# State-space factors held without their empty halves and multiplied in 64 by 64 pieces; attention's near and far values joined by a transpose and an addition

## The chip, the cores and the metric

One core of a Trainium2 chip runs the whole kernel. The metric is the device time of one execution in microseconds (us), taken as the median of several. The core has five engines that work through their own queues of instructions in order: PE (TensorE, matrix products; the loading of its weights is listed apart as PEld), DVE (VectorE), ACT (ScalarE), POOL (GpSimd) and SP (which here only issues transfers). Products go into PSUM, a memory of eight banks of 128 by 512 fp32 numbers, and DVE and ACT copy them out.

## The reference, cut to what matters

One block of a hybrid network on 512 tokens of width 1024, in fp32:

```
z = rms_norm(x) @ w_in                       # state-space input, q, k, v, two gates
y_a = s5_mixer(z[:, :512]) @ w_branch_a      # 32 groups of 16 channels, 64 complex states each
y_b = dilated_attention(q, k, v) @ w_branch_b
h = x + (g_a * y_a + g_b * y_b) @ w_out
h = h + conv-gated feed-forward(h);  h = h + per-layer gate(h, p);  return rms_norm(h)

# s5_mixer: per group g and state p, with a = exp(lambda * dt)
s[t] = a * s[t-1] + bbar @ u[t]              # complex
y[t] = Re(c @ s[t]) + d * u[t];  y = gelu(y);  y = y * sigmoid(y @ glu_w + glu_b)

# dilated_attention: 12 heads in three groups; a query's output joins, over the three groups,
# sums of exp(score) * value over the last 128 tokens, over every 4th and over every 16th token
```

## The kernel before, in words

**Layout.** The 512 tokens are held as four residues (token modulo 4) of 128. The large products are done in fp32r as three products, high by high, high by low and low by high part (`mm3`, L149 to L151; 3168 products of 128x128 weights, nearly all by 512 columns). Their weights come in chunks of 128x1024 over SP's queue; ACT makes the high part (`wh`, L128) and DVE the low part (`wl`, L129), three buffers each.

**The background work.** Two generators, `g_ssm` (state space) and `g_attn` (attention), issue their instructions between the large products; after every few products `tick` lets them go on for a budget of estimated cost, which each `yield` states. A scheduler with priorities then fixes each engine's order when the program is built, so on the chip each queue is a fixed list. Small products of both take PSUM tiles of one bank from a pool of three (`ax_tile`); the large ones have five more.

**State space.** Tokens are taken in 128 blocks of four. The 32 groups stand in 16 pairs; a pair's two groups of 64 states fill 128 partitions. The factors of the recurrence within a block are built on DVE (`expand`): `BD[i]` (i is the real or imaginary plane) maps a pair's inputs (2 groups by 4 taps by 16 channels) to its states. As one group's inputs do not touch the other group's states, half of each 128x128 factor is zero; POOL writes the zeros (`zero`, L587) and ACT copies the two filled 64-row halves in (L601). Then on PE:

- `g1t` (L616): 32 transposes of `BD`, 128x128 each, copied by ACT to `G1` (L617).
- `hps` (L627): 32 products of `BD` with the output factors, 128x32 weights by 128 columns, which give the response within a block; DVE copies them (L628), four transposes `hp` turn them, DVE adds them to the direct term `Hm`, and three products `shp` (L645) shift them to make the matrix `T`.
- `ut` (L658): 16 transposes of the input, copied by ACT to `U`.
- `es` (L671): 32 products of `G1` with `U`, 128x128 by 128 columns, the input's share of each block's end state; ACT copies each bank in two pieces to `E`, one block late (L673, L674).
- DVE then runs the recurrence over the 128 blocks in place in `E` (`cstep`; it also rebuilds the factors as `G2`).
- `ys` (L721 to L723): per pair three products, `U` by `T` and `E` by both planes of `G2`, then gelu on ACT.

**Attention.** Eight steps of two heads and 128 queries, each followed by 24 large products of the gates (`gps`): scores (L766, L771), softmax on DVE and ACT, transposes of the probabilities (L796, L798). The values of the two sparse groups come out with queries on partitions (`values`, L817; DVE copies them to `ao`), those of the near group with channels on partitions (`far_values`, L828). `finish_values` (L834) multiplies `ao` by the identity and lets PSUM add it to the near values; ACT and DVE then split the sum into its high and low parts `bh` and `bl`.

After `ys`, the attention and the gates the rest is large products in a row, with no background work.

Of the kernel before, what the change touches and what calls it, by code (L numbers as in the profile page):

```python
# [17 lines left out]
P = 128  # L18
# [3 lines left out]
R = 4  # L22
NQ = 16
H = 16
# [40 lines left out]
def tile_hybrid_block(ctx: ExitStack, tc: tile.TileContext, xT, xtok, pT, W, vecs, consts, ssm, out):  # L65
    nc = tc.nc
    ACT, DVE, POOL, PE = nc.scalar, nc.vector, nc.gpsimd, nc.tensor
# [4 lines left out]
    ring = ctx.enter_context(tc.tile_pool(name="ring", bufs=3))  # L72
# [3 lines left out]
    def slot(i, shape, name, dt=F32):  # L76
        return sb.tile([P] + shape, dt, tag=f"s{i}", name=name)
# [7 lines left out]
    def ax_tile(name):  # L85
        return px.tile([P, 512], F32, tag="ax", name=name)
# [105 lines left out]
    ident = cst[:, C_ID:C_ID + 128]  # L192
# [231 lines left out]
    def g_ssm():  # L424
# [123 lines left out]
        for e in range(2, 5):  # L548
            o = (pn(), pn())
# [30 lines left out]
        ncim = pz[:, 4]  # L580
        Hm = pz[:, 5]
# [4 lines left out]
        def zero(t):  # L586
            POOL.memset(t, 0.0)  # L587

        def expand(dst, ex, plane, e0, re, im, sgn):
# [7 lines left out]
            tt(w[:, 1], imb, pi if plane == 0 else pr, ALU.mult)  # L597
            tt(w[:, 0], w[:, 0], w[:, 1], ALU.subtract if plane == 0 else ALU.add)
# [8 lines left out]
        BD = [slot(f"g{i}", [NQ, 2, R, H], f"BD{i}") for i in range(2)]  # L607
        G1 = [slot(f"f{i}", [NQ, P], f"G1{i}") for i in range(2)]
        for i in range(2):
            zero(BD[i])  # L610
            yield from expand(BD[i], ex, i, 1, bb[:, 0], bb[:, 1], 1.0)
        for i in range(2):
            for q4 in range(4):
                ps = ax_tile("g1t")
                for q in range(4):
                    PE.transpose(ps[:, q * 128:(q + 1) * 128], flat(BD[i], q4 * 4 + q), ident)  # L616
                ACT.activation(G1[i][:, q4 * 4:q4 * 4 + 4, :].rearrange("p q m -> p (q m)"), ps, AF.Copy)  # L617
                yield 0.15


        hT = slot("U", [4, P], "hT")
        hps = ax_tile("hps")
        for q in range(NQ):
            q0 = min(q, NQ - 2)
            o = hps[(q % 4) * 32:(q % 4) * 32 + 32, (q // 4) * 128:(q // 4 + 1) * 128]
            for i, cc in enumerate((c_re, ncim)):
                PE.matmul(o, cc[:, q0:q0 + 2, :].rearrange("p q h -> p (q h)"), flat(BD[i], q), start=(i == 0), stop=(i == 1))  # L627
# [5 lines left out]
        hv = hp2.rearrange("p (q h) -> p q h", h=32)  # L633
        tt(Hm, cst[:, C_DI:C_DI + 16].unsqueeze(1).to_broadcast([P, NQ, H]), sp[:, S_D:S_D + 16].unsqueeze(2).to_broadcast([P, NQ, H]), ALU.mult)
        tt(Hm[:, 0:15], Hm[:, 0:15], hv[:, 0:15, 0:16], ALU.add)
        tt(Hm[:, 15:16], Hm[:, 15:16], hv[:, 15:16, 16:32], ALU.add)
        T = slot("T", [NQ, 2, R, H], "T")
        zero(T)
        Hf = Hm.rearrange("p q h -> p (q h)")
# [11 lines left out]

        while "s_done" not in env:
            yield None
        U = slot("U", [NQ, P], "U")
        for q4 in range(4):
            ps = ax_tile("ut")
            for q in range(4):
                PE.transpose(ps[:, q * 128:(q + 1) * 128], flat(S, q4 * 4 + q), ident)  # L658

            ACT.activation(U[:, q4 * 4:q4 * 4 + 4, :].rearrange("p q (i b) -> p q i b", i=4),  # L660
                           ps.rearrange("p (q b i) -> p q i b", q=4, i=4), AF.Copy)
            yield 0.15
        E = slot("x", [2, NQ, P], "E")
        E4 = E.rearrange("p i q (f b) -> p i q b f", f=4)
        E16 = E.rearrange("p i q (f s g) -> p i q s g f", f=4, g=4)
        DVE.memset(E[:, :, :, 0:1], 0.0)
        for i in range(2):
            for q4 in range(4):
                ps = ax_tile("es")
                for q in range(4):  # L670
                    PE.matmul(ps[:, q * 128:(q + 1) * 128], G1[i][:, q4 * 4 + q, :], U[:, q4 * 4 + q, :], start=True, stop=True)  # L671
                psq = ps.rearrange("p (q c) -> p q c", q=4)
                ACT.activation(E[:, i, q4 * 4:q4 * 4 + 4, 32:128], psq[:, :, 0:96], AF.Copy)  # L673
                ACT.activation(E[:, i, q4 * 4:q4 * 4 + 4, 1:32], psq[:, :, 96:127], AF.Copy)  # L674
                yield 0.15

        G2 = [slot(f"g{i}", [NQ, 2, R, H], f"G2{i}") for i in range(2)]
        ex2 = slot("f1", [2048], "ex2")
# [36 lines left out]
        Yg = slot("S", [R, 32, H], "Yg")  # L715
        for q4 in range(4):
            ps = ax_tile("ys")
            for q in range(4):
                qq = q4 * 4 + q
                o = ps[:, q * 128:(q + 1) * 128]  # L720
                PE.matmul(o, U[:, qq, :], flat(T, qq), start=True, stop=False)  # L721
                PE.matmul(o, E[:, 0, qq, :], flat(G2[0], qq), start=False, stop=False)
                PE.matmul(o, E[:, 1, qq, :], flat(G2[1], qq), start=False, stop=True)  # L723
# [14 lines left out]
    def g_attn():  # L738
# [83 lines left out]
        def far_values(n, ov, pT_):  # L822
            t, hp = n // 2, n % 2
            nb = 2 if t else 1
            for b in range(nb):
                for a in range(2):
                    h = 2 * hp + a
                    PE.matmul(ov[halves[a], 0:128], V[:, t - nb + 1 + b, h * 64:(h + 1) * 64], pT_[:, a, 2 + b, :],  # L828
                              start=(b == 0), stop=False, skip_group_check=True)

        def finish_values(n, ov, ao):

            t, hp = n // 2, n % 2
            PE.matmul(ov[:, 0:128], ao, ident, start=False, stop=True, skip_group_check=True)  # L834
            ov3 = ov[:, 0:128].rearrange("p (r i) -> p r i", r=R)
            bhv, blv = tile_of(bh[:, hp], t), tile_of(bl[:, hp], t)
            ACT.activation(bhv, ov3, AF.Copy)
            tt(blv, ov3, bhv.bitcast(F32), ALU.subtract)

# [85 lines left out]
    h = slot("x", [KD, SEQ], "h")  # L925
# [25 lines left out]
    for m in range(KD):  # L951
        ps = mm_tile("ops")
# [10 lines left out]
    for part in range(2):  # L963
# [4 lines left out]
        for mi in range(HALF):  # L968
# [23 lines left out]
        for m in range(KD):  # L992
            ps = mm_tile("dps")
# [13 lines left out]
    for m in range(KD):  # L1007
        ps = mm_tile("pps")
# [31 lines left out]
    for m in range(KD - NLAST):  # L1040
        ps = mm_tile("eps")
# [48 lines left out]
    n = 0  # L1090
    for rs, y in zip(LAST, y4):
        for j in range(2):
            for r in rs:
# [3 lines left out]
                o = fo[r // 2][:, r % 2, j * 512:(j + 1) * 512]  # L1097
# [52 lines left out]
def _layout(inputs):  # L1150
# [22 lines left out]
    def add(t):  # L1173
        parts.append(t.transpose(1, 0, 2).reshape(128, -1))
# [3 lines left out]
    def tok(c0, n):  # L1178
        add(w_in[:, c0:c0 + n].reshape(8, 128, n))

    tok(0, 512)
    tok(2304, 512)
    for j in range(3):
        tok(512 + 512 * j, 512)
# [34 lines left out]
    dd = np.broadcast_to(f["ssm_d"][0].reshape(16, 2, 1, 16), (16, 2, 4, 16)).reshape(16, 128).T  # L1219
# [26 lines left out]
```

## Time and profile before

| | us |
|---|---|
| median of 3 runs | 797.88 (796.67 to 797.92) |
| profiled execution, its own time | 797.59 |
| its span, first to last instruction | 795.8 |
| PE busy in the span | 786.5 (99%) |
| DVE busy | 494.1 (62%) |
| ACT busy | 346.5 (44%) |

The page's first part gives busy time by engine, its second part the span in 40 slices of 19.9 us with the busy share in tenths. An fp32 product appears in PE's records as two records, a transpose and an fp32r product as one. Records overlap, since a product is some 0.16 us or more in the array after the next has begun: what a product takes of PE's time is the distance from its start to the next one's start, not the length of its record.

### The profile page before, as it was taken

To read this page: it belongs to the slowest core of one execution; us is meant where nothing else is said; L and a number is where in the kernel's file an instruction comes from. 1 tells how busy PE (TensorE), PEld (TensorE's weight loads), DVE (VectorE), ACT (ScalarE), POOL (GpSimd) and SP (SyncE) were. 2 spreads that over 40 slices of the span, in tenths; PEclk is the share of its full clock that TensorE was granted. 3 is DMA by queue.
4 is the path that set the end of the run, shared out by engine and by line. 5 is a ranking of instruction groups with operands and counts; after the bars stand their busy time and mean duration, and the time that the engine had idled before them with its cause. 6 is when DMAs were issued, how large, how long until landed. Compare 5 with 4: busy or idle time off the path is not lost.

```text
span 795.8 us, 10898 instructions
## 1 busy us (share of the span) xinstructions
PE 786.5 (99%) x4302; PEld 650.6 (82%) x4302; DVE 494.1 (62%) x960; ACT 346.5 (44%) x551; POOL 10.9 (1%) x10
## 2 busy tenths in 40 slices
PE   8999999999999999999999999999999999999996
PEld 6888888888777788888888888888888888888886
DVE  6974799943566558656856555233566565455576
ACT  5763643445445443435534433212334333335464
POOL 2001000000000000000000000000000000000000
PEclk9999999999999999999999999999999999999999
DMA  7731122231121122633222332332322322322302
GB/s 268 272 104 54 54 80 80 81 107 54 61 73 55 54 105 83 209 106 110 103 98 87 107 103 82 106 102 84 106 89 97 106 95 90 106 91 94 106 1 107
DMA packets 23811, 78.99 MB, mean 99 GB/s; under 512 B 2640, under 2 KB 3024, under 8 KB 23760
## 3 DMA queue, kind: packets, MB, share of 16 engines
q1 hardware_dynamic: 23616, 78.22, 28.9%
q8 instruction: 34, 0.56, 0.3%
q14 instruction: 17, 0.14, 0.1%
q10 hardware_dynamic: 144, 0.07, 0.0%
HBM read 76.18 MB, written 2.10 MB: 98 GB/s over the span
## 4 chain that ended last, share of the span: by engine, by line
PE 94%; ACT 2%; DVE 2%; issue 1%; DMA 1%; SPq 0%; DVEq 0%; ACTq 0%
PE pg L151 5%; PE dps L151 5%; PE pu L151 5%; PE dps L150 5%; PE pu L150 5%; PE pu L149 5%; PE pg L150 5%; PE pg L149 5%; PE dps L149 5%; PE pa L151 4%; PE pa L150 4%; PE pa L149 4%; PE gps L149 4%; PE gps L151 4%; PE gps L150 4%; PE ops L151 2%
## 5 line engine op out<-in xcount | busy, mean ns | idle before, releaser
L128 ACT ACTIVATE wh<-wr 128x1024 fp32r<-128x1024 f32 (+1 forms) x132 | 138.2, 1047 | 293.9 <-issue 64.6
L129 DVE TENSOR_TENSOR wl<-wr,wh 128x1024 fp32r<-128x1024 f32 (+1 forms) x132 | 159.1, 1206 | 67.6 <-ACT wh L128 67.4
L150 PE MATMUL pu<-u2l,wh 128*128 128x512 f32 x176 | 68.5, 389 | 0.0
L149 PE MATMUL pu<-u2h,wh 128*128 128x512 f32 x176 | 68.5, 389 | 0.0
L151 PE MATMUL pg<-u2h,wl 128*128 128x512 f32 x176 | 68.5, 389 | 0.0
L149 PE MATMUL pg<-u2h,wh 128*128 128x512 f32 x176 | 68.5, 389 | 0.0
L150 PE MATMUL pg<-u2l,wh 128*128 128x512 f32 x176 | 68.5, 389 | 0.0
L149 PE MATMUL dps<-ah,wh 128*128 128x512 f32 x176 | 68.5, 389 | 0.0
L150 PE MATMUL dps<-al,wh 128*128 128x512 f32 x176 | 68.5, 389 | 0.0
L151 PE MATMUL dps<-ah,wl 128*128 128x512 f32 x176 | 68.5, 389 | 0.0
L151 PE MATMUL pu<-u2h,wl 128*128 128x512 f32 x176 | 68.5, 389 | 0.0
L149 PE MATMUL pa<-wh,u1h 128*128 128x512 f32 x160 | 63.0, 396 | 1.5 <-ACT u1h L159 1.5
L150 PE MATMUL pa<-wl,u1h 128*128 128x512 f32 x160 | 62.8, 393 | 0.0
L151 PE MATMUL pa<-wh,u1l 128*128 128x512 f32 x160 | 62.4, 392 | 0.1
L149 PE MATMUL gps<-u1h,wh 128*128 128x512 f32 x128 | 51.1, 399 | 0.0
L151 PE MATMUL gps<-u1h,wl 128*128 128x512 f32 x128 | 50.1, 391 | 0.0
L150 PE MATMUL gps<-u1l,wh 128*128 128x512 f32 x128 | 49.9, 390 | 0.0
L413 DVE TENSOR_TENSOR ext<-pg,n_y 128x512 f32<-128x512 f32 x22 | 15.2, 692 | 44.1 <-PE pg L151 44.1
L150 PEld LDWEIGHTS pg<-u2l,wh 128*128 128x128 f32 x176 | 33.0, 188 | 6.9
L150 PEld LDWEIGHTS dps<-al,wh 128*128 128x128 f32 x176 | 33.0, 188 | 6.9
L150 PEld LDWEIGHTS pu<-u2l,wh 128*128 128x128 f32 x176 | 33.0, 188 | 6.9
L149 PEld LDWEIGHTS dps<-ah,wh 128*128 128x128 f32 x176 | 33.0, 188 | 6.9
(305 smaller groups left out, 1497.3 us busy)
## 6 DMA issues: line engine op xcount, KB each, us to landing
wr<-in_W_dram SPq DMA_DIRECT2D x128, 512.0 KB, 3.2
xt<-in_xtok_dram SPq DMA_DIRECT2D x4, 512.0 KB, 7.7
h<-in_xT_dram SPq DMA_DIRECT2D x8, 256.0 KB, 5.4
out_dram<-fo SPq DMA_DIRECT2D x8, 256.0 KB, 2.3
x<-in_xT_dram SPq DMA_DIRECT2D x7, 256.0 KB, 6.1
wr<-in_W_dram SPq DMA_DIRECT2D x4, 256.0 KB, 5.7
cst<-in_consts_dram SPq DMA_DIRECT2D x1, 568.0 KB, 10.2
sp<-in_ssm_dram SPq DMA_DIRECT2D x1, 544.0 KB, 7.7
```

The lines of the kernel that those rows point to most:

```text
L128: ACT.activation(hi[:, c], raw[:, c], AF.Copy)
L129: DVE.tensor_tensor(lo[:, c], raw[:, c], hi[:, c].bitcast(F32), op=ALU.subtract)
L149: PE.matmul(ps, st[0], mv[0], start=first, stop=False)
L150: PE.matmul(ps, st[0], mv[1], start=False, stop=False)
L151: PE.matmul(ps, st[1], mv[0], start=False, stop=last)
L413: DVE.tensor_tensor(o, a, b, op=op)
```

## The change

Part one keeps `BD` without its zero halves (half the size), so that DVE writes it directly and the zeroing and ACT's copies go; `g1t` becomes 16 transposes, each of two groups' filled blocks. `hps` becomes 64 products with 64 rows, 32 weight columns and 64 columns each, and `es` 64 products of 64x64 weights by 128 columns. The pieces of `es` are issued two from one PSUM bank and two from the next in turn, so that three banks are in use at a time; ACT and DVE copy the banks in turn. The shift by one block moves from `E` to `U`, which gets 32 leading columns that DVE fills from PSUM. For the groups to meet on the same partitions the second and third of every four groups change places in the columns of `w_in` and in `d`; the products of `T` write to the permuted places. Part two replaces the product of `ao` with the identity by a transpose into a free part of the same bank; ACT copies the near values out and DVE adds the two before the split.

```diff
-        for i in range(2):
-            zero(BD[i])
-            yield from expand(BD[i], ex, i, 1, bb[:, 0], bb[:, 1], 1.0)
+            w = products(ex, i, 1, bb[:, 0], bb[:, 1])
+            tt(BD[i], w[:, 0], w[:, 1], ALU.subtract if i == 0 else ALU.add)
...
-            for q4 in range(4):
+            for q4 in range(2):
                 ps = ax_tile("g1t")
                 for q in range(4):
-                    PE.transpose(ps[:, q * 128:(q + 1) * 128], flat(BD[i], q4 * 4 + q), ident)
+                    x0 = 2 * (q4 * 4 + q)
+                    PE.transpose(ps[:, q * 128:(q + 1) * 128], BD[i][:, x0:x0 + 2].rearrange("p k t h -> p (k t h)"), ident)
...
+        for a in range(4):
+            for e in range(2):
+                for k in range(2):
+                    for j in range(2):
+                        sl = 32 * (2 * e + j)
+                        o = hps[sl:sl + 32, a * 128 + k * 64:a * 128 + k * 64 + 64]
+                        q0 = 2 * (2 * a + e)
+                        for i, cc in enumerate((c_re, ncim)):
+                            PE.matmul(o, cc[halves[j], q0:q0 + 2, :].rearrange("p q h -> p (q h)"),
+                                      BD[i][halves[j], q0 + k].rearrange("p t h -> p (t h)"), start=(i == 0), stop=(i == 1),
+                                      skip_group_check=True)
...
+        Hm5 = Hm.rearrange("p (a e j) h -> p a e j h", a=4, e=2)
+        for k in range(2):
+            for e in range(2):
+                tt(Hm5[halves[k], :, e], Hm5[halves[k], :, e], hv[halves[k], :, e, :, k, :], ALU.add)
...
+            DVE.tensor_copy(Ux[:, q4 * 4:q4 * 4 + 4, 1:32], ps.rearrange("p (q b i) -> p q i b", q=4, i=4)[:, :, 3, 0:31])
...
-        for i in range(2):
-            for q4 in range(4):
-                ps = ax_tile("es")
-                for q in range(4):
-                    PE.matmul(ps[:, q * 128:(q + 1) * 128], G1[i][:, q4 * 4 + q, :], U[:, q4 * 4 + q, :], start=True, stop=True)
-                psq = ps.rearrange("p (q c) -> p q c", q=4)
-                ACT.activation(E[:, i, q4 * 4:q4 * 4 + 4, 32:128], psq[:, :, 0:96], AF.Copy)
-                ACT.activation(E[:, i, q4 * 4:q4 * 4 + 4, 1:32], psq[:, :, 96:127], AF.Copy)
+        banks = [(i, q4, k) for i in range(2) for q4 in range(2) for k in range(2)]
+        def part(n, which):
+            ...
+            return [(pss[n][halves[j], q * 128:(q + 1) * 128], G1[i][halves[k], q4 * 4 + q, halves[j]],
+                     Ux[halves[k], 2 * (q4 * 4 + q) + j, 0:P]) for q in (2 * which, 2 * which + 1) for j in range(2)]
+        for n in range(len(banks) + 1):
+            now, nxt_ = part(n - 1, 1), part(n, 0)
+            for c in range(0, 4, 2):
+                for o, g, u_ in now[c:c + 2] + nxt_[c:c + 2]:
+                    PE.matmul(o, g, u_, start=True, stop=True, skip_group_check=True)
+            if now:
+                ...
+                if n % 2:
+                    ACT.activation(o, pv_, AF.Copy)
+                else:
+                    DVE.tensor_copy(o, pv_)
...
-            PE.matmul(ov[:, 0:128], ao, ident, start=False, stop=True, skip_group_check=True)
-            ov3 = ov[:, 0:128].rearrange("p (r i) -> p r i", r=R)
+            PE.transpose(ov[:, 256:384], ao, ident)
+            bs = ring.tile([P, 128], F32, tag="bs", name="bs", bufs=2)
+            ACT.activation(bs, ov[:, 0:128], AF.Copy)
+            tt(bs, ov[:, 256:384], bs, ALU.add)
```

The built order moves with it. On PE, before, from the last transposes of the input to the first large products after `es` (`pa` is a large product of the q, k and v projection, of which 24 make a chunk of weights):

```order
305 L658 MATMUL ut<-cst,S 128x128 x12
306 L149 MATMUL pa_647<-wh_942,u1h_89 128x512
307 L658 MATMUL ut<-cst,S 128x128 x4
308 L671 MATMUL es<-U,G_568 128x128 x16
309 L671 MATMUL es<-U,G_569 128x128 x16
310 L150 MATMUL pa_647<-wl_943,u1h_89 128x512
```

The same place on PE in the changed kernel:

```order
313 L663 MATMUL shp<-pz,cst 128x256
314 L680 MATMUL ut<-cst,S 128x128 x8
315 L149 MATMUL pa_641<-wh_919,u1h_89 128x512
316 L680 MATMUL ut<-cst,S 128x128 x4
317 L150 MATMUL pa_641<-wl_920,u1h_89 128x512
...
321 L680 MATMUL ut<-cst,S 128x128 x4
322 L708 MATMUL es<-U,G_568 64x128 x30
323 L708 MATMUL es<-U,G_569 64x128 x2
324 L708 MATMUL es<-U,G_568 64x128 x2
325 L708 MATMUL es<-U,G_569 64x128 x18
...
345 L708 MATMUL es<-U,G_569 64x128 x12
```

`es` now begins after the 245th large product and not after the 265th, 20 products sooner, and its last 12 pieces stand behind 19 further large products.

On DVE, before, at the same place (`scr` and `ex` are the recurrence's and the factors' scratch):

```order
154 L649 COPY T<-pz 64x16x16 x2
155 L649 COPY T<-shp 64x16x16 x2
156 L129 TENSOR_TENSOR wl_1022<-wr_1020,wh_1021 128x1024
157 L649 COPY T<-shp 64x16x16 x4
158 L129 TENSOR_TENSOR wl_1088<-wr_1086,wh_1087 128x1024
159 L413 TENSOR_TENSOR scr<-E,apw 128x512 x2
160 L413 TENSOR_TENSOR ex_933<-sp,apw 128x1024 x2
```

and on DVE in the changed kernel:

```order
153 L667 COPY T<-shp 64x16x16 x6
154 L129 TENSOR_TENSOR wl_1054<-wr_1052,wh_1053 128x1024
155 L684 COPY U<-ut 128x4x31 x4
156 L716 COPY E<-es 128x4x128 x2
157 L413 TENSOR_TENSOR scr<-E,apw 128x512 x2
158 L716 COPY E<-es 128x4x128
159 L129 TENSOR_TENSOR wl_1120<-wr_1118,wh_1119 128x1024
160 L716 COPY E<-es 128x4x128
161 L413 TENSOR_TENSOR ex_965<-sp,apw 128x1024 x2
```

DVE now stands between PE's banks and their next use: four copies of `U` and four of `E` were added, with two of the recurrence's instructions and one weight split among them. Later on PE, all four groups of `ys` now stand together after the 600th large product; before, two stood there and two after the 624th.

## Rows read from the trace of the kernel before

**Rows 1.** The page: busy time by engine, then PE and DVE in 40 slices.

```profile
PE 786.5 (99%) x4302; PEld 650.6 (82%) x4302; DVE 494.1 (62%) x960; ACT 346.5 (44%) x551; POOL 10.9 (1%) x10
...
PE   8999999999999999999999999999999999999996
...
DVE  6974799943566558656856555233566565455576
```

**Rows 2.** The page: the chain that ended last, shares of the span by engine.

```profile
PE 94%; ACT 2%; DVE 2%; issue 1%; DMA 1%; SPq 0%; DVEq 0%; ACTq 0%
```

**Rows 3.** Waits of PE: who waited for whom, us in total, times, longest.

```profile
PE pa L149 <- ACT u1h L159: 1.5, 3, 0.7
PE warm L165 <- DVE apw L526: 1.0, 1, 1.0
```

**Rows 4.** Timeline of PE, 57.2 to 64.6: start us, length us, line, count.

```profile
57.30 0.39 PE L150 MATMUL pa<-wl,u1h 128*128 128x512 f32 x1
57.52 0.39 PE L151 MATMUL pa<-wh,u1l 128*128 128x512 f32 x1
57.76 1.47 PE L616 MATMUL g1t<-cst,BD 128*128 128x128 f32 x12
58.98 0.48 PE L149 MATMUL pa<-wh,u1h 128*128 128x512 f32 x1
59.60 2.61 PE L616 MATMUL g1t<-cst,BD 128*128 128x128 f32 x20
62.14 0.45 PE L627 MATMUL hps<-BD,sp 128*32 128x128 f32 x8
...
64.09 0.50 PE L150 MATMUL pa<-wl,u1h 128*128 128x512 f32 x1
```

**Rows 5.** Tile es: duration ns min/median/max, first and last start us, forms.

```profile
L671 PE MATMUL es<-U,G x64: 275/275/370, 79.0 to 86.1; 128*128 128x128 f32 x64
```

**Rows 6.** Timeline of PE in one attention step, 214.9 to 218.4.

```profile
216.57 0.70 PE L766 MATMUL sc<-qk,qk 64*128 64x256 f32 x4
217.20 0.46 PE L771 MATMUL sc<-qk,qk 64*32 64x64 f32 x32
217.58 0.44 PE L828 MATMUL ov<-pts,V 128*64 128x128 f32 x4
217.95 0.49 PE L834 MATMUL ov<-cst,ao 128*128 128x128 f32 x2
218.20 0.48 PE L149 MATMUL gps<-u1h,wh 128*128 128x512 f32 x1
```

**Rows 7.** Tile g1t: ACT's copies of one bank.

```profile
L617 ACT ACTIVATE G<-g1t x8: 579/617/661, 59.0 to 62.3; 128x512 f32<-128x512 f32 x8
```

**Rows 8.** Tile hps: DVE's copy of one bank.

```profile
L628 DVE COPY hT<-hps x1: 692/692/692, 64.2 to 64.2; 128x512 f32<-128x512 f32 x1
```

**Rows 9.** Tile ov: the split's DVE half, 128x128.

```profile
L413 DVE TENSOR_TENSOR bx<-ov,bx x8: 280/284/292, 204.5 to 272.5; 128x128 fp32r<-128x128 f32 x8
```

**Rows 10.** Waits of DVE at the end of es.

```profile
DVE scr L413 <- ACT E L674: 4.3, 1, 4.3
...
DVE ex L413 <- PE es L671: 1.6, 1, 1.6
```

**Rows 11.** Timeline of all engines, 155 to 190: the recurrence's last writes, the first ys.

```profile
160.40 2.48 DVE L413 TENSOR_TENSOR E<-E,scr 128x992 f32<-128x992 f32 x3
...
169.38 0.38 PE L721 MATMUL ys<-T,U 128*128 128x128 f32 x2
```

**Rows 12.** Stretches: span us, then busy time of PE, PEld, DVE, ACT, POOL (instructions), clock, DMA share, GB/s.

```profile
86.00:163.00 77.00, 76.91 (x367) 63.53 (x367) 75.96 (x221) 35.97 (x59) 0.00 (x0) 1.00 0.22 76
...
188.00:272.00 84.00, 84.00 (x918) 64.86 (x919) 47.10 (x108) 39.49 (x92) 1.48 (x1) 1.00 0.17 58
```

More of the change, by code (lines that the diff above doesn't have):

```diff
@@ L587, in zero, with products @@
             POOL.memset(t, 0.0)
-        def expand(dst, ex, plane, e0, re, im, sgn):
+        def products(ex, plane, e0, re, im):
             pr = apw[:, 0, e0:e0 + 4, :].rearrange("p e q -> p q e").unsqueeze(3).to_broadcast([P, NQ, R, H])
@@ L597, in expand @@
             tt(w[:, 1], imb, pi if plane == 0 else pr, ALU.mult)
+            return w
+        def expand(dst, ex, plane, e0, re, im, sgn):
+            w = products(ex, plane, e0, re, im)
             tt(w[:, 0], w[:, 0], w[:, 1], ALU.subtract if plane == 0 else ALU.add)
@@ L605, in flat @@
             return t[:, q].rearrange("p j t h -> p (j t h)")
-        BD = [slot(f"g{i}", [NQ, 2, R, H], f"BD{i}") for i in range(2)]
-        G1 = [slot(f"f{i}", [NQ, P], f"G1{i}") for i in range(2)]
+        NP = NQ // 2
+        BD = [slot(f"g{i}", [NQ, R, H], f"BD{i}") for i in range(2)]
+        G1 = [slot(f"f{i}", [NP, P], f"G1{i}") for i in range(2)]
         for i in range(2):
-            zero(BD[i])
-            yield from expand(BD[i], ex, i, 1, bb[:, 0], bb[:, 1], 1.0)
+            w = products(ex, i, 1, bb[:, 0], bb[:, 1])
+            tt(BD[i], w[:, 0], w[:, 1], ALU.subtract if i == 0 else ALU.add)
+            yield 2.8
         for i in range(2):
-            for q4 in range(4):
+            for q4 in range(2):
                 ps = ax_tile("g1t")
                 for q in range(4):
-                    PE.transpose(ps[:, q * 128:(q + 1) * 128], flat(BD[i], q4 * 4 + q), ident)
+                    x0 = 2 * (q4 * 4 + q)
+                    PE.transpose(ps[:, q * 128:(q + 1) * 128], BD[i][:, x0:x0 + 2].rearrange("p k t h -> p (k t h)"), ident)
                 ACT.activation(G1[i][:, q4 * 4:q4 * 4 + 4, :].rearrange("p q m -> p (q m)"), ps, AF.Copy)
@@ L622, in g_ssm @@
         hps = ax_tile("hps")
[L623 to L627, printed above, removed]
+        for a in range(4):
[9 more added lines that the diff above has]
+                                      skip_group_check=True)
         DVE.tensor_copy(hT.rearrange("p a m -> p (a m)"), hps)
@@ L653, in g_ssm @@
             yield None
-        U = slot("U", [NQ, P], "U")
+        Ux = slot("U", [NQ, 32 + P], "U")
+        U = Ux[:, :, 32:32 + P]
+        DVE.memset(Ux[:, :, 0:1], 0.0)
         for q4 in range(4):
@@ L661, in g_ssm @@
                            ps.rearrange("p (q b i) -> p q i b", q=4, i=4), AF.Copy)
+            DVE.tensor_copy(Ux[:, q4 * 4:q4 * 4 + 4, 1:32], ps.rearrange("p (q b i) -> p q i b", q=4, i=4)[:, :, 3, 0:31])
             yield 0.15
         E = slot("x", [2, NQ, P], "E")
+        EP = E.rearrange("p i (q k) c -> p i q k c", k=2)
         E4 = E.rearrange("p i q (f b) -> p i q b f", f=4)
         E16 = E.rearrange("p i q (f s g) -> p i q s g f", f=4, g=4)
-        DVE.memset(E[:, :, :, 0:1], 0.0)
-        for i in range(2):
-            for q4 in range(4):
-                ps = ax_tile("es")
-                for q in range(4):
-                    PE.matmul(ps[:, q * 128:(q + 1) * 128], G1[i][:, q4 * 4 + q, :], U[:, q4 * 4 + q, :], start=True, stop=True)
-                psq = ps.rearrange("p (q c) -> p q c", q=4)
-                ACT.activation(E[:, i, q4 * 4:q4 * 4 + 4, 32:128], psq[:, :, 0:96], AF.Copy)
-                ACT.activation(E[:, i, q4 * 4:q4 * 4 + 4, 1:32], psq[:, :, 96:127], AF.Copy)
-                yield 0.15
+        banks = [(i, q4, k) for i in range(2) for q4 in range(2) for k in range(2)]
+        pss = {}
+        def part(n, which):
+            if not 0 <= n < len(banks):
+                return []
+            i, q4, k = banks[n]
+            if which == 0:
+                pss[n] = ax_tile("es")
+            return [(pss[n][halves[j], q * 128:(q + 1) * 128], G1[i][halves[k], q4 * 4 + q, halves[j]],
[6 more added lines that the diff above has]
+            if now:
+                i, q4, k = banks[n - 1]
+                o = EP[:, i, q4 * 4:q4 * 4 + 4, k]
+                pv_ = pss.pop(n - 1).rearrange("p (q c) -> p q c", q=4)
+                if n % 2:
+                    ACT.activation(o, pv_, AF.Copy)
+                else:
+                    DVE.tensor_copy(o, pv_)
+            yield 0.15
         G2 = [slot(f"g{i}", [NQ, 2, R, H], f"G2{i}") for i in range(2)]
@@ L718, in g_ssm @@
             for q in range(4):
+                o = ps.rearrange("p (q k j c) -> p q j k c", q=2, k=2, j=2)[:, q // 2, q % 2]
+                PE.matmul(o, U[:, q4 * 4 + q, :], T[:, q4 * 4 + q].rearrange("p k t h -> p k (t h)"), start=(q == 0), stop=False,
+                          skip_group_check=True)
+            for q in range(4):
                 qq = q4 * 4 + q
                 o = ps[:, q * 128:(q + 1) * 128]
-                PE.matmul(o, U[:, qq, :], flat(T, qq), start=True, stop=False)
-                PE.matmul(o, E[:, 0, qq, :], flat(G2[0], qq), start=False, stop=False)
-                PE.matmul(o, E[:, 1, qq, :], flat(G2[1], qq), start=False, stop=True)
+                PE.matmul(o, E[:, 0, qq, :], flat(G2[0], qq), start=False, stop=False, skip_group_check=True)
+                PE.matmul(o, E[:, 1, qq, :], flat(G2[1], qq), start=False, stop=True, skip_group_check=True)
             ACT.activation(
@@ L1179, in tok @@
         add(w_in[:, c0:c0 + n].reshape(8, 128, n))
-    tok(0, 512)
+    add(w_in[:, :512].reshape(8, 128, 8, 2, 2, 16).transpose(0, 1, 2, 4, 3, 5).reshape(8, 128, 512))
     tok(2304, 512)
@@ L1218, in _layout @@
     dtr = np.broadcast_to(f["ssm_log_dt"][0][:, None], (32, 64))
-    dd = np.broadcast_to(f["ssm_d"][0].reshape(16, 2, 1, 16), (16, 2, 4, 16)).reshape(16, 128).T
+    dd = np.broadcast_to(f["ssm_d"][0].reshape(8, 2, 2, 16).transpose(1, 3, 0, 2)[:, None], (2, 4, 16, 8, 2)).reshape(128, 16)
     ssm = np.concatenate([gp(f["ssm_lam_re"][0]), gp(f["ssm_lam_im"][0]), gp(dtr), dd,
```

11 lines of the change are left out of this document (5 added, 6 removed).

## The prediction

> **What bounds the kernel now.** I read the page's first part, then the chain that ended last, then PE's waits. PE is busy 786.5 of 795.8 us [rows 1], the chain runs over PE for 94% [rows 2], and PE's own waits come to 2.5 us in four pieces, all of them for the first operands of the kernel [rows 3]. Between the first and the last slice PE is never under nine tenths [rows 1]. So PE's queue is the length of the kernel: time that a PE instruction no longer takes comes off the end, unless PE then waits for something that was early so far. What could be late is DVE: from 86 to 163 us it is busy 75.96 of 77.0 us with the recurrence, in the attention only 47.1 of 84 [rows 12]. What follows the attention has no part in the change.
>
> I take PE's time by distances between starts, not by the length of records. A plain large product takes 57.52 - 57.30 = 0.22 to 0.23 us [rows 4].
>
> **The change part by part, PE first.**
>
> *Transposes g1t.* Before, 12 take 58.98 - 57.76 = 1.22 us and 20 take 62.14 - 59.60 = 2.54 us [rows 4], together 3.76 us or 0.117 each. 16 of 32 go: **-1.9 us**. Beside them four of ACT's eight copies, four 64-row copies into the factors and two of POOL's fills go; they lay beside PE and count for nothing.
>
> *hps.* Before, 32 products leave 64 records and take 64.09 - 62.14 = 1.95 us, 0.030 each [rows 4], whereas a 128-column record with 128x128 weights takes (86.1 - 79.0)/63 = 0.113 [rows 5]: four column groups already work at once. After, 128 records have half the columns, so 0.056 each alone. The order goes over two tiles (upper rows with column group 0, lower rows with group 1), back, and then over the other two; if four are at work, it is 128 x 0.056/4 = 1.8, and with two changes between tiled and whole array (1.95 less 64 x 0.113/4, so 0.07 each) 1.9 to 2.1. Bounds from rows: at the rate of the 64x32 scores, 32 records in 217.58 - 217.20 = 0.38 us, 0.012 each [rows 6], it would be 1.5 (-0.4); one tile at a time, 7.2 (+5.2). I take 2.0: **+0.05 us**.
>
> On the floor under small products the row speaks first: 32 score records of 64 columns start 0.012 us apart [rows 6]. The Trainium skill, in "TensorE: Matmul & The Clock Gate", section "Wait — 56ns, not 53.3ns?", says that start-to-start never drops below about 25 ns, however small the product; by that hps would take 128 x 0.025 = 3.2 us and the sum be 1.2 us worse. The trace does not agree, and the row decides.
>
> *es.* Before: 64 records in 7.15 us [rows 5]. After, 128 records of 128 columns. No row shows 64x64 weights. The nearest: four tiles of 128x32, 0.030 a record [rows 4]; two tiles of 128x64, four records in 217.95 - 217.58 = 0.37 us, and two tiles of 64x128, four records of 256 columns in 217.20 - 216.57 = 0.63 us, where alone they would take 4 x 0.22 [rows 6]. Row halves and column groups both run side by side there, so I take four at a time: 0.028 a record, 0.45 us for a step of eight pieces. That alone would be 3.9 us (-3.2). But there are only three banks. A bank's last result comes 0.16 us after its slot (record of 0.275 against 0.113), the copy takes 0.617 on ACT [rows 7] or 0.692 on DVE [rows 8], with the semaphores I estimate 0.9 us from the last slot to a free bank. A step can begin only 0.9 us after the end of the step before the last, so two steps take 0.45 + 0.9 = 1.35, not 0.9. The first three steps (1.35 us) do not meet this, the next four take 0.68 each (2.7), the last two (0.9) are put behind 19 large products, in which the banks come free; four changes of tiling add 0.3. That is 5.25 us, of which I take 5.4: **-1.75 us**. Ends: -3.2 with no wait, and one tile at a time 128 x 0.113 = 14.4, +7.3.
>
> *Joining the values.* The product with the identity takes 218.20 - 217.95 = 0.25 us for two records [rows 6]; the transpose leaves one record, as in g1t 0.117. Eight times: **-1.0 us**. ACT copies 128x128 and DVE adds 128x128, about 0.28 us each [rows 9], 2.3 us on each over eight steps. They lie beside the 24 gate products of each step (24 x 0.227 = 5.4 us), with DVE at 56% and ACT at 47% there [rows 12]; the bank of `ov` is wanted again only behind them. Without that cover it would be 0.56 us a step, 4.5 us in all.
>
> *ys* keeps its 48 products; only their order and place move. No change.
>
> *New waits of PE.* Ahead of `shp`, six large products (1.4 us) and not 19 now cover four DVE additions of some 0.28 us and a result's 0.16. Ahead of `es`, `U` passes through ACT's 0.617 and then a DVE copy of 124 columns, behind a weight split on DVE. Four large products lie there. Each of these comes out within 0.2 us of even, so I take **+0.3 us** together, with 0 and 0.8 as ends.
>
> *DVE.* Four copies of `E` (4 x 0.69) and four small ones are added, about 3.7 us. DVE had idle time just there: 4.3 us until the first `E`, 1.6 us until PE was through `es` [rows 10]. Since `es` starts 20 large products (4.5 us) sooner, and 1.9 us sooner for g1t, its last pieces, 19 large products later, end near 82.6 us where they ended at 86.2, so the recurrence starts about 3 us sooner. Its last write ended at 160.40 + 2.48 = 162.9, and PE came for it at 169.4 [rows 11]: 6.5 us of room. PE comes 4.3 us sooner, the write about 3; some 5 us of room stay.
>
> **Sum.** -1.9 + 0.05 - 1.75 - 1.0 + 0.3 = -4.3 us. On the profiled execution's 797.59 that gives 793.3. That execution lies 0.3 under the median of the runs, 797.88, so for a median I say **793.6 us**.
>
> **The rivals.**
>
> *The banks do not bind* (chance 0.16). ACT and DVE free the banks as fast as PE fills them, the small waits are nil, and es takes 3.9 us: 1.5 + 0.3 less, -6.1, **791.8**. For it: PE never waits for a bank in the trace [rows 3]. Against: the 0.9 us above are mostly the copy's own measured length.
>
> *DVE comes late to the banks* (0.10). Every second bank waits for DVE, which has a weight split of 1.22 us and the recurrence's pairs in its queue; es then stays at some 7.1 us and the waits at 0.8: -2.1, **795.8**. For it: the order puts two instructions of the recurrence ahead of the third copy. Against: that copy's bank is not wanted again within es.
>
> *hps one tile at a time* (0.07). In hps the upper and lower 64 rows write to one bank, which they never do in the trace (the scores go to a bank for each half). If two row halves shut each other out in a bank, neighbours in the order can't run together, and hps takes 7.2 us: -4.3 + 5.2, +0.9, **798.8**, no change. The Trainium skill, in "TensorEngine Tiling (Array Packing)", section "Gotcha 1: PSUM Pressure", says that different row tiles cannot access the same PSUM bank at once. No row here shows whether that holds where they write different partitions. es is laid over two banks and is not touched by it.
>
> *es one tile at a time* (0.05), the other side. If pieces with 64x64 weights run one after another, each record takes 0.113 us: es becomes 14.4 us, and all in all -4.3 + 1.75 + 7.3 = +4.7 us, **802.6**. It decides from the point where a record takes more than about (5.4 + 4.3)/128 = 0.076 us, so where fewer than 1.5 pieces run at once. For it: no row has this shape, and the pairs with 64 rows gain only a third. Against: the 64x32 scores run at 0.012.
>
> **How the numbers follow.** The forecast has 0.62, good for 792.4 to 795 with its own bounds. A measurement of this kernel tells 0.2%, 1.6 us, from no change; that is 796.3 below and 799.5 above. Forecast and first rival are faster, the second mostly is: 0.62 + 0.16 + 0.08 = 0.86. Same: the rest of the second, and hps, 0.09. Slower: es serial, 0.05. The range runs from 791.4, just past the first rival, to 796.6, past the second; it leaves out the last two and some of the edges, under 0.2.
>
> **What would show it.** Right: 24 records fewer of g1t and `ov` (16 and 8), worth 2.9 us by starts; es with groups of four records 7 to 15 ns apart, gaps of 0.2 to 0.5 us from the fourth bank on, 5 to 6 us in all; hps at 2 us; PE with no wait at the first ys. Wrong: records of es or hps evenly 0.05 or 0.11 us apart; PE waiting for DVE at ys or in the attention; or a PE that is idle for the weights' high and low parts, which now stand elsewhere in ACT's and DVE's queues. The forecast fails if a gain on PE does not come off the end, which would show as PE idle time in the later slices.

## The result, and the profile after

Measured: 793.16 us, median of the changed kernel, against 797.5 before; ratio 0.9945, interval 0.9934 to 0.9957. The forecast was 793.6. The profile of those runs fell into an execution with a lower clock, so rows of "after" come from the same kernel run again:

> The changed kernel once more, for a profile at the full clock. My theory (the gain is PE time taken out of its queue, part by part): -4.3 us against the kernel before; starts on PE show g1t 1.9 us, es 5 to 6 us in two pieces with gaps from the fourth bank on, hps 1.9 to 2.1 us, the joining transpose 0.12 us a step, and the new waits ahead of shp and es together under 0.8 us. Rival (the banks do not bind): es near 3.9 us. Rival (something else gives the gain): these terms by starts do not add up to the difference of the two spans.

It took 793.0 us (792.76 to 793.24; before in the same session 797.3; ratio 0.9943, 0.9931 to 0.9955). Its page, busy time by engine and PE's slices, against [rows 1], and the chain that ended last, against [rows 2]:

```profile
PE 782.4 (99%) x4406; PEld 645.7 (82%) x4406; DVE 498.0 (63%) x978; ACT 340.5 (43%) x539; POOL 7.4 (1%) x8
...
PE   9999999999999999999999999999999999999996
...
PE 95%; ACT 2%; DVE 2%; DMA 1%; issue 0%; SPq 0%; DVEq 0%; ACTq 0%
```

PE is still the length of the kernel: 786.5 - 782.4 = 4.1 us less of it. Its span fell by 4.8, from 795.8 to 791.0; the other 0.8 lies ahead of the 24th large product, in the input's arrival: that product starts at 12.46 us before and at 11.67 here. In the other profiles it starts 0.1 to 0.9 us sooner than before, also where the kernel's start is the same, so I do not put this part down to the change.

PE's waits, against [rows 3] (us, times, longest): both belong to the kernel's start, and none to `shp`, `es`, `ys` or the attention.

```profile
PE warm L165 <- DVE apw L526: 1.1, 1, 1.1
PE pa L149 <- ACT u1h L159: 0.6, 1, 0.6
```

PE's weight loads have a wait at `yt` that the kernel before does not have, for a copy that frees a bank:

```profile
PEld yt L779 <- ACT yT L780: 0.4, 1, 0.4
```

PE from g1t to the end of hps, against [rows 4]; columns start, length, line, count:

```profile
57.00 1.47 PE L625 MATMUL g1t<-cst,BD 128*128 128x128 f32 x12
58.22 0.48 PE L149 MATMUL pa<-wh,u1h 128*128 128x512 f32 x1
58.79 0.66 PE L625 MATMUL g1t<-cst,BD 128*128 128x128 f32 x4
59.38 0.31 PE L640 MATMUL hps<-BD,sp 64*32 64x64 f32 x4
59.51 0.28 PE L640 MATMUL hps<-BD,pz 64*32 64x64 f32 x4
...
61.84 0.50 PE L150 MATMUL pa<-wl,u1h 128*128 128x512 f32 x1
```

g1t takes 1.22 + 0.59 = 1.81 us, where it took 3.76. hps takes 61.84 - 59.38 = 2.46 us, where it took 1.95: it became longer.

`es`, its copies, and what ACT and DVE stood idle for ahead of these (the tile's view; durations min/median/max; idle us and times), against [rows 5]:

```profile
L708 PE MATMUL es<-U,G x128: 269/269/320, 72.3 to 81.9; 64*64 64x128 f32 x128
L714 ACT ACTIVATE E<-es x4: 582/597/598, 73.4 to 82.2; 128x512 f32<-128x512 f32 x4
L716 DVE COPY E<-es x4: 681/687/692, 73.9 to 83.5; 128x512 f32<-128x512 f32 x4
its engine sat idle before it (us, times) until:
  PE es L708: 2.8, 5
```

By starts, without the 19 large products between its two pieces, `es` takes 5.29 us (7.16 before). The last line says that ACT and DVE, too, waited for PE, five times, 2.8 us in all: neither copying engine is full, so what may bind is the round of a bank, filled and then copied, not the copies' sum. The experiments on `es` below ask that.

One attention step, against [rows 6]:

```profile
217.29 0.66 PE L875 MATMUL ov<-pts,V 128*64 128x128 f32 x8
217.88 0.33 PE L881 MATMUL ov<-cst,ao 128*128 128x128 f32 x1
217.96 0.48 PE L149 MATMUL gps<-u1h,wh 128*128 128x512 f32 x1
```

The join takes 217.96 - 217.88 = 0.08 us, where the product took 0.25: over the eight steps 0.67 instead of 1.95, -1.28.

The recurrence's last writes and the first `ys` that reads them, against [rows 11]:

```profile
157.86 2.48 DVE L413 TENSOR_TENSOR E<-E,scr 128x992 f32<-128x992 f32 x3
...
166.48 0.39 PE L769 MATMUL ys<-G,E 128*128 128x128 f32 x2
```

The write ends at 160.34, PE comes 6.1 us later.

### The profile page after: what moved, and what is told of

Same layout as the page of the kernel before. It is cut to its first block, busy times and chain, and to the rows that moved or that the text cites. A ratio compares the mean times of both kernels' runs of the same rounds, so it can differ in the third digit from the quotient of the medians.

```text
span 975.7 us, 11103 instructions
## 1 busy us (share of the span) xinstructions
PE 968.1 (99%) x4406; PEld 691.8 (71%) x4406; DVE 500.9 (51%) x978; ACT 343.3 (35%) x539; POOL 7.4 (1%) x8
## 4 chain that ended last, share of the span: by engine, by line
PE 99%; DMA 0%; DVE 0%; ACT 0%; DVEq 0%; issue 0%
PE pg L151 5%; PE dps L150 5%; PE pu L149 5%; PE dps L149 5%; PE pu L151 5%; PE dps L151 5%; PE pu L150 5%; PE pg L149 5%; PE pg L150 5%; PE pa L151 5%; PE pa L149 5%; PE pa L150 5%; PE gps L149 4%; PE gps L150 4%; PE gps L151 4%; PE eps L150 2%
## 5 line engine op out<-in xcount | busy, mean ns | idle before, releaser
L149 PE MATMUL pu<-u2h,wh 128*128 128x512 f32 x176 | 80.6, 458 | 0.0
L150 PE MATMUL pu<-u2l,wh 128*128 128x512 f32 x176 | 80.6, 458 | 0.0
L150 PE MATMUL dps<-al,wh 128*128 128x512 f32 x176 | 80.4, 457 | 0.0
L151 PE MATMUL pu<-u2h,wl 128*128 128x512 f32 x176 | 80.4, 457 | 0.0
L151 PE MATMUL pg<-u2h,wl 128*128 128x512 f32 x176 | 80.4, 457 | 0.0
L151 PE MATMUL dps<-ah,wl 128*128 128x512 f32 x176 | 80.3, 456 | 0.0
L149 PE MATMUL pg<-u2h,wh 128*128 128x512 f32 x176 | 80.3, 456 | 0.0
L149 PE MATMUL dps<-ah,wh 128*128 128x512 f32 x176 | 80.1, 455 | 0.0
L413 DVE TENSOR_TENSOR up<-pu,n_y 128x512 f32<-128x512 f32 x22 | 15.2, 691 | 67.3 <-PE pu L151 67.3
L151 PEld LDWEIGHTS pu<-u2h,wl 128*128 128x128 f32 x176 | 35.4, 201 | 14.8
```

What stands on the lines that cost most here:

```text
L149: PE.matmul(ps, st[0], mv[0], start=first, stop=False)
L150: PE.matmul(ps, st[0], mv[1], start=False, stop=False)
L151: PE.matmul(ps, st[1], mv[0], start=False, stop=last)
```

## The experiments

Ratios are against the kernel before, run in the same session (medians 797.2 to 797.3).

**One part at a time.** Part two alone, on the kernel before:

> The kernel before with part two alone (transpose and addition in place of the product with the identity). My theory: -1.0 us, 0.117 to 0.13 us of PE a step, with ACT's copy and DVE's addition wholly covered. Rival (the longer chain over ACT and DVE is not covered): no gain or a loss, up to 0.56 us a step, +3.5 us, with PE idle in the attention.

Measured 797.35 us, ratio 1.0001 (0.9992 to 1.0009): no gain, where I had expected 1.0 us. Yet the join's records have become shorter as in the full change, and from the 24th to the last large product PE takes 1.32 us less than before. The gain is lost behind that: from the start of the last large product to the end of the span it is 11.38 us before and 12.78 with part two alone, 1.4 more. The output transfers on SP's queue, before and then with part two alone:

```profile
787.70 4.80 SPq L1103 DMA_DIRECT2D out_dram<-fo  x8
```

```profile
785.97 5.75 SPq L1106 DMA_DIRECT2D out_dram<-fo  x8
```

The eight issues begin 1.7 us sooner (0.4 of it from the input's arrival) and take 0.95 longer. In the trace the third of them, which takes 0.33 us before, takes 1.68, and the page's median from issue to landing is 3.3 us instead of 2.3. At 787.0, 0.26 us ahead of that issue, a 16 KB packet of the instruction queue q8 starts. The DMA view from 786.8 to 788.5:

```profile
q1 hardware_dynamic: 270, 0.49, 75.9%
q8 instruction: 1, 0.02, 5.8%
```

Where large products stand in a row, such packets come every 123 to 133 of PE's records, some 29 us, so I take them for PE's instructions. Before, the last came at 786.2, alone in its stretch, 1.5 us ahead of the first output transfer. Part two takes 8 of PE's records away, so what follows stands elsewhere in that rhythm. To test it I made PE's list as long as before again:

```diff
+            PE.transpose(ov[0:32, 384:416], ident[0:32, 0:32], ident[0:32, 0:32])
             PE.transpose(ov[:, 256:384], ao, ident)
```

> The kernel before with part two alone, and 8 further transposes of 32x32 constants on TensorE, one ahead of each step's transposing of ao, into a free part of the bank. They leave the order of everything else as in the run of part two alone, but make TensorE's list of instructions as long as before, so that its last instruction fetch falls back to where it was before, ahead of the output transfers. Theory (the gain of part two was lost to a fetch that met the third output transfer): no long issue on SyncE, and 796.3 us (795.9 to 796.7): 1.28 us gained less 8 small transposes of some 0.02 us. Rival, the gain goes in another way, and the late output transfer follows from the 1.3 us by itself: 797.5 us with the issue of 1.7 us still there.

Measured 797.0 us (0.9987 to 1.0005). The total lies outside the 795.9 to 796.7 that I had expected; the trace shows what the theory said. The packet comes at 785.0, and the issues take their usual time:

```profile
786.55 4.81 SPq L1107 DMA_DIRECT2D out_dram<-fo  x8
```

The total misses by what I put in. One step of this kernel:

```profile
217.06 0.20 PE L834 MATMUL ov<-cst 32*32 32x32 f32 x1
217.19 0.33 PE L835 MATMUL ov<-cst,ao 128*128 128x128 f32 x1
```

The small transpose holds PE for 0.13 us, not 0.02: 1.05 us over eight steps. 797.3 - 1.28 + 1.05 = 797.1, as measured. The 0.35 us between the two medians are within the noise; the profiles tell it: the stretch behind the last large product is 11.36 us again, 1.4 us less than with part two alone. Moving the packet moved the loss. The twelve traces used here, one execution of each kernel, agree: in ten of them, in which no instruction packet starts between the first output issue and the last landing, that stretch takes 11.36 to 11.38 us; it is longer only with part two alone and in the next run, which have one there. What the packet and the transfers share is not shown.

Part one alone (the join as before):

> The kernel before with the state-space part alone, the join of the values left as it was (product with the identity). If the two parts add on TensorE, the join gives back the 1.28 us that its records show, and the time is 794.3 us (793.9 to 794.8), its trace 1.3 us later than the changed kernel's from the last attention step to the end. Rival, the join is worth nothing in the total, as the run with it alone had it: 793.0 us. Rival, this program's end meets the same slow output transfer as that run did (an instruction fetch of TensorE that falls between the output transfers): 795.6 us with one issue on SyncE of some 1.7 us.

Measured 795.06 us, ratio 0.9969 (0.9958 to 0.9981): 2.1 us over the full change, more than the join's 1.28 and over the 794.8 that I had allowed. From the 24th to the last large product it gains 2.54 us on before, the full change 4.04; the difference, 1.5, is the join to 0.2. The rest lies behind the last large product: 11.91 us instead of 11.37, and the last output transfer lands 3.24 us after its issue began instead of 2.69. An 8 KB packet of the other instruction queue, q14, falls there (790.2). Its part in that was not tested.

**hps.** Its neighbours in the list:

```diff
-            for e in range(2):
-                for k in range(2):
-                    for j in range(2): ...
-                        for i, cc in enumerate((c_re, ncim)):
+            for k in range(2):
+                for i, cc in enumerate((c_re, ncim)):
+                    for e in range(2):
+                        for j in range(2): ...
```

> The changed kernel with the 64 products hps in another order: the four products that stand on different quarters of the array (both halves of the rows, all four groups of 32 columns) follow each other, and the two products that add into one place stand four apart rather than one behind the other. All else keeps its order. Theory (hps costs 2.45 us because two neighbours in its list stand on the same tile): hps falls to 1.9 to 2.0 us, 792.6 us (792.3 to 792.9). Rival, products on several tiles that write into one bank hinder each other, and neighbours on different tiles make it worse: hps at 2.5 to 4 us, 793.1 to 794.6 us.

Measured 792.66 us (792.47 to 792.8; 0.9927 to 0.9952). PE at hps:

```profile
59.73 0.32 PE L640 MATMUL hps<-BD,sp 64*32 64x64 f32 x8
59.87 0.29 PE L640 MATMUL hps<-BD,pz 64*32 64x64 f32 x8
...
61.43 0.29 PE L640 MATMUL hps<-BD,pz 64*32 64x64 f32 x8
61.65 0.50 PE L150 MATMUL pa<-wl,u1h 128*128 128x512 f32 x1
```

61.65 - 59.73 = 1.92 us, where the change's own order takes 2.46. The distances of the records' starts, in ns, changed order of the experiment first:

```
hps, new order:      7  7  6 60 |  7  7  6 36 |  7  7  6 36 |  7  6  7 36
hps, as changed:    13 67 13 43 | 13 43 13 42 | 14  6 13 23 | 30 14 12  1
```

In the new order four start together every 56 ns, and that in one bank with both row halves, which write different partitions of it: row halves do not shut each other out there.

**es: banks or products?** Three kernels change the copies and the banks, two the order of the products. First each bank's copy split between ACT and DVE:

```diff
-                if n % 2:
-                    ACT.activation(o, pv_, AF.Copy)
-                else:
-                    DVE.tensor_copy(o, pv_)
+                ACT.activation(o[:, 0:2], pv_[:, 0:2], AF.Copy)
+                DVE.tensor_copy(o[:, 2:4], pv_[:, 2:4])
```

> The changed kernel, but each bank of es is copied half by ACT and half by DVE at the same time, not whole by one of them in turn. If the time from a bank's last slot to a free bank bounds es, that time falls from 0.9 to some 0.6 us, two steps take 1.05 us in place of 1.35, and es in its first piece and with it the kernel gets 0.6 us shorter than the changed kernel. Rival (banks do not bind, or DVE's queue ahead of its copies binds): 0, or a loss of up to 0.5 us, since DVE now stands behind every bank.

Measured 794.23 us (0.9946 to 0.9971): 1.2 us worse, not 0.6 better. The copies of this kernel, and two waits that are new, one of DVE and one of PE:

```profile
L713 ACT ACTIVATE E<-es x8: 367/384/385, 73.5 to 83.0; 128x256 f32<-128x256 f32 x8
L714 DVE COPY E<-es x8: 415/420/425, 73.9 to 84.3; 128x256 f32<-128x256 f32 x8
```

```profile
DVE E L714 <- ACT E L713: 1.3, 3, 0.5
PE qkT L392 <- ACT qk L400: 0.7, 1, 0.7
```

The two halves were not copied at the same time, as I had meant them to be: in all eight banks DVE's half starts only after ACT's half has ended, 0.03 to 0.04 us later where DVE stood idle. So a bank is held for 0.384 + 0.04 + 0.420 = 0.84 us of copying, where one engine alone takes 0.597 or 0.687. `es` took 5.69 us, 0.40 more. That is the theory tested the other way round: a bank held some 0.2 us longer makes `es` longer. The wait at `qkT` is most likely the further work put on ACT (eight halves are 3.1 us, four whole banks 2.4); this was not tested. Next, banks freed sooner without more work on ACT and DVE; GpSimd fills the other half of `E` from `U`, so this kernel leaves half of the end states out:

```diff
-                    ACT.activation(o, pv_, AF.Copy)
+                    ACT.activation(o[:, 0:2], pv_[:, 0:2], AF.Copy)
...
+                POOL.tensor_copy(o[:, 2:4], Ux[:, 0:2, 0:P])
```

> The changed kernel, but ACT and DVE copy only the first half of each es bank (256 columns, some 0.38 and 0.42 us rather than 0.60 and 0.69); GpSimd writes the other half of E from U, so half of the end states are not those of the reference. A bank is free some 0.25 us earlier. Theory of the prediction (the loop of three banks, filled in turn and copied, sets the pace of es, 0.66 us a bank): a bank's loop gets 0.25 us shorter, a bank some 0.08 us, es falls from 5.29 to 4.6 us (4.3 to 4.9). Rival (the products themselves set the pace): es stays at 5.2 to 5.4 us. The total is not what is asked; GpSimd's copies may move the recurrence.

`es` fell to 4.81 us, as expected (the total to 792.76, which the missing half makes no measure of the change). Then a fourth bank, with hps in its new order:

```diff
-                pss[n] = ax_tile("es")
+                pss[n] = (mm_tile if n % 4 == 3 else ax_tile)("es")
```

> The changed kernel with hps in the other order, and every fourth bank of es taken from the large products' five banks, of which four are in use there: four banks in turn rather than three. The order on all engines stays. Theory (three banks bind): es falls from 5.29 to 4.0 to 4.6 us, the time to 791.7 us (791.3 to 792.1) beside 792.66 with hps alone. Rival (the products bind): es 5.3 us, 792.7 us. Rival, the fifth bank is not free when es wants it: es longer than 5.3 us or a wait of a large product, 792.7 to 794 us.

Measured 791.85 us (791.44 to 792.18), ratio 0.9931 (0.9918 to 0.9943): the fastest of all kernels here, 0.8 us under hps alone. `es` took 4.48 us:

```profile
72.44 3.52 PE L708 MATMUL es<-U,G 64*64 64x128 f32 x104
...
80.46 1.10 PE L708 MATMUL es<-U,G 64*64 64x128 f32 x24
```

Both say the banks bind; the fourth one gives back 0.8 of the 5.29 us. Next the interleaving of two banks:

```diff
-            now, nxt_ = part(n - 1, 1), part(n, 0)
-            for c in range(0, 4, 2): ...
+            for o, g, u_ in (part(n - 1, 0) + part(n - 1, 1) if n else []): ...
```

> The changed kernel, but the 8 pieces of a bank are issued one after another and not two and two from two banks. They all have one half of the rows, so two tiles work at a time and not four, if neighbours in the order decide it: 0.9 us a bank in place of 0.45, es some 7.3 us in all as in the kernel before, +1.8 us against the changed kernel. Rival (PE looks far enough ahead in its queue to mix the next bank's pieces in, or the banks bound it anyway): within 0.5 us of the changed kernel.

Measured 793.21 us (0.9932 to 0.9959), `es` 5.43 us: 0.14 worse, where I had expected 1.8. The rival held, that PE mixes the next bank's products in by itself: the record that carries the wait for the second bank is the 11th to start, though the loop puts the first bank's 16 records ahead of it. Last, four products of one quarter of the array behind one another:

```diff
-            now, nxt_ = part(n - 1, 1), part(n, 0)
-            for c in range(0, 4, 2): ...
+            now = part(n - 1, 0) + part(n - 1, 1)
+            for o, g, u_ in now[0::2] + now[1::2]:
+                PE.matmul(o, g, u_, start=True, stop=True, skip_group_check=True)
```

> The changed kernel with the products of es in the order of their place in the array: the four of a bank that stand on one quarter (64 rows, 64 columns) one after another, then the four of the bank's other quarter, bank after bank. Theory (products overlap only with neighbours on another quarter; one behind the other on one quarter takes 0.21 us each, twice 128 rows by two records at the clock of 2.4 GHz, as the 112 ns a record of es before bear out): runs of four cost 0.65 us each, es 10.4 us (9 to 11.5), 798.1 us (796.8 to 799.3). Rival (quarters do not matter, the pace is that of the banks or of the queue): es 5.3 us, 793.1 us.

Measured 796.82 us (0.9986 to 1.0003). By starts `es` takes 6.44 us for its first 96 records and 8.93 in all, just under the 9 that I had expected at least:

```profile
72.88 6.51 PE L707 MATMUL es<-U,G 64*64 64x128 f32 x96
79.32 0.50 PE L151 MATMUL pa<-wh,u1l 128*128 128x512 f32 x1
```

So quarters do count: their order alone is worth 3.6 us, and 3.5 beside the kernel with one bank in a row, which differs only in the order within a bank. A run of four took 0.54 us, not 0.65, since the next quarter's run starts beside its second half. Cuts from the starts, in ns:

```
es, as changed, from the 16th record on: 39  7 56  7 39 | ... |  7 102  7 102  7 102
es, four banks:                           7 56  7 39 | 7 56  7 39 | 7 57  6 39
es, one bank in a row, two cuts:           6 103  6 103  7 101  8 102 | ... | 6 57  6 40 | 7 56  6 40
es, quarter after quarter:              109  6 103 57 52 57 53 56 | 109  6 103 57 ...
```

109 ns is a record alone on its quarter, about as long as one on the whole array (112 in the kernel before). In 109 ns either four records start or two. I read the four as two banks at hand and the two as one, since one bank holds only two quarters' products. The counts bear it out: of the 124 places from which four further starts can be followed, those come within 0.12 us in 48 with three banks, 66 with half copies and 84 with four banks. The loop's interleaving adds nothing to that: with one bank in a row it is 48 too. Quarter after quarter it is 0.

**DVE's room at ys.** Thirteen operations more on DVE, ahead of `ys`:

```diff
+        for _ in range(13):
+            tt(E[:, 0, 0:4], E[:, 0, 0:4], E[:, 0, 0:4], ALU.max)
```

> The changed kernel with 13 further VectorE operations of 128x512 (elementwise maximum of a part of E with itself, 0.69 us each, 9.0 us in all) between the recurrence and the products ys; the order on TensorE is not changed. Theory of the prediction (VectorE has some 5 us of room before the first ys): about 4 us of the 9 come out as a wait of TensorE at the first ys, 797.0 us (795.5 to 799.0). Rival, VectorE's end of the recurrence is nowhere near the bound (more than 9 us of room): 793.1 us, no wait at ys. Rival, there is no room at all: 802 us.

Measured 801.87 us (1.0042 to 1.0067): 8.9 over the changed kernel and outside the 795.5 to 799.0 that I had expected. It looks as if there had been no room at all, but PE waited for only part of it:

```profile
PE ys L771 <- DVE E L413: 6.2, 1, 6.2
```

```profile
166.00:172.50 6.50, 1.51 (x11) 1.23 (x9) 6.33 (x10) 1.67 (x2) 0.00 (x0) 1.00 0.35 122
172.50:178.00 5.50, 4.26 (x20) 4.29 (x21) 2.80 (x4) 2.48 (x3) 0.00 (x0) 0.53 0.35 114
```

The second fence is two stretches (columns as in [rows 12], the clock third from the end). In the second, in which PE comes back from standing idle, the granted clock was 0.53, near the lower level of 1.2 GHz, and PE's first `ys` pairs there started 0.43 us apart instead of 0.22. `ys` takes 9.3 us more, 6.2 of wait and some 3 of this; I had not reckoned with it. The wait itself is 9.0 us of additions, plus 3.8 of DVE's other work that stood among them (two weight splits and two of the gates' operations, 2 x 1.21 + 2 x 0.68), less 6.2: 6.6 us of room, beside the 6.1 that the changed kernel's rows show.

## Why the prediction was right, and where it was not

The sum was right: -4.3 foretold, 797.3 to 793.0 measured, and PE's records give -4.04 from the 24th product on. That it fits better than its terms is luck: hps came out 0.45 worse, the join and es together 0.4 better. Its terms:

- **g1t**: -1.9 foretold, -1.95 measured. The 0.117 us a transpose held; nothing beside it came to the surface.
- **hps**: +0.05 foretold, +0.50 measured: the term most in error. The step that failed is "if four are at work": I read four tiles from the loop, but the loop puts two products for the same tile behind each other. With four different neighbours it took 1.92, within the 1.9 to 2.1 that I had. The rivals' price of 7.2 us for a bank shared by row halves did not come; nor did the Trainium skill's rule in "TensorEngine Tiling (Array Packing)", section "Gotcha 1: PSUM Pressure", show here: four records of both row halves, on different partitions of one bank, start 7 ns apart. Nor does the floor of 25 ns between starts from the Trainium skill's "TensorE: Matmul & The Clock Gate", section "Wait — 56ns, not 53.3ns?": 7 ns again.
- **es**: -1.75 foretold, -1.87 measured, by the mechanism foretold: three banks bind (copies that hold a bank longer 5.69, half copies 4.81, four banks 4.48). The look of it was wrong. I expected groups of four and then gaps of 0.2 to 0.5 us; instead there is one gap of 0.19 us, and PE otherwise goes on with fours or with pairs, two records in 109 ns. And my bound without bank waits, 3.9 us, was not reached with four banks.
- **The join**: -1.0 foretold, -1.28 measured: a transpose behind tiled products takes 0.084 us, not g1t's 0.117. The bookkeeping "comes off the end" held in the full change (11.37 us behind the last large product, 11.38 before), but not for this part alone, whose 1.28 us went into a late transfer issue that nothing in the profile of before announced.
- **New waits**: +0.3 foretold ahead of `shp` and `es`, where next to nothing came (`shp` +0.03, `ut` +0.04). What is left of PE's sum, -4.04 against the -4.60 of the four terms, is +0.6 all the same: +0.27 at `yt`, by the wait for a bank that its weight loads show and that I had not foreseen, and +0.2 on large products beside small ones, whose cause was not tested. That the size came near is luck too.
- **DVE's room**: 5 us foretold, 6.1 by the rows, 6.6 by the experiment. The 6.5 us of before were read from a product of `T` and `U`, which does not read `E`; the first that does starts 0.2 later, at 169.60.

Of the rivals, "the banks do not bind" fell by the two experiments, "DVE late to the banks" by `es` at 5.29, "hps one tile at a time" by hps at 2.46. "es one tile at a time" fell too; when forced, it cost 3.6 us and not the 9 I had priced: PE runs ahead into the next quarter, and pairs still ran side by side.

## What to carry to other kernels

Small products on parts of the array are worth what their neighbours in the list are: let each follow one on another part, and let as many banks be open as it takes to offer all parts; 0.5 us in hps and 0.8 in es were still to be had so. PE looked ahead by a few products itself, so giving up the interleaving of two banks cost only 0.14 us, but runs of four on one quarter cost 3.6. Before a rate is read from a row, look at which tiles the neighbours stand on. A copy split between two engines is not yet a copy done by both at once: look in the trace at when the second half starts. And a gain on the bounding engine shows in the total only if the tail behind it repeats: compare the last output transfers before calling a part worthless.

## What the runs showed of the hardware that I had not expected

- An instruction packet of 16 KB that started 0.26 us ahead of an output transfer's issue went with an issue of 1.68 us instead of 0.33; moved 2 us away, the issue was normal again. The stretch behind the last large product was 12.78 us with it, 11.36 to 11.38 in the ten traces without an instruction packet among the output transfers.
- A 32x32 transpose behind 128x64 products held PE for 0.13 us, more than the 128x128 transpose after it (0.085).
- A record of 128 columns on 64x64 weights takes 109 ns alone (112 on 128x128 weights); up to four such share that time.
- PE starts products of the next bank, on other quarters, ahead of earlier ones in its list: with one bank in a row the second bank's first record was the 11th to start, not the 17th.
- PE stood idle for 6.2 us, up to 173.7; over 172.5 to 178.0 the granted clock was 0.53.
